# Moving the weight, token and feature buffers of a TensorE-bound layer to chosen remainders of 256 bytes

## The chip, the cores and the metric

The kernel runs on one core of a Trainium2 chip. The time is device microseconds of one execution. Three runs of the kernel before gave 2293.25, 2295.34 and 2296.85 us; the median, 2295.34 us, is the time before.

## The reference

One layer of a streaming encoder on 2048 prompt tokens and 8 x 16 sample tokens, 2176 rows of 1024 values in fp32. What matters here are its four large matrix products; between them stand two kinds of attention, norms and a gate.

```python
z = x @ w_in                                  # 1024 -> 2824
mix = concatenate([mlstm(z), window_attention(z)]) @ w_out     # 1024 -> 1024
h = layer_norm(ALPHA * x + mix)
u = h @ w_up                                  # 1024 -> 5632 (value | gate)
c = b_conv + sum(ext[:, j:j + T] * w_conv[j] for j in range(3))
y = layer_norm(ALPHA * h + (silu(gate) * value) @ w_down)      # 2816 -> 1024
```

## The kernel before

**Exactness and products.** Each fp32 operand is split into a high part that TensorE takes exactly (float32r) and the remainder, by `split` (L216 to L219): ScalarE writes the high part, VectorE the low part. A product is then three matmuls: high x high, high x low, low x high. The three largest stages (input, up and down projection) save an eighth of the blocks by a Strassen-like scheme of seven products, numbered 1 to 7, on sums and differences of quarter blocks. Where the text says "product 3", it is the `s` of the code.

**Order.** TensorE's order is written out by hand (`manual_schedule` for PE). DMAs are issued almost all on SyncE's queue. GpSimd's own queue issues 44: in the mLSTM chain a row of maxima to DRAM and back, broadcast (L1089, L1091), and 12 row blocks of the result `y` (L2133). GpSimd's transfers have a scratch in SBUF of 4096 bytes in every partition, the first thing in the memory (`dynamic_dma_scratch_size`, in `kernel`).

**Stages.**
- Input projection: four blocks of token tiles, five groups of columns. `i_product` (L701 on, matmuls at L713) streams tokens `oh`/`ol` against loaded weights `w` for groups 0 and 1 and streams weights against loaded tokens for groups 2 to 4, 256 columns each. The gate columns (264 wide) are made in `i_direct` (L739). The chains of both attentions are woven in between.
- Output projection: `group`, whose matmuls are recorded at L223 to L225 in `mm3`: the tokens are loaded, 512 columns of weights stream. One tile of 128 tokens takes eight steps of three matmuls; each two steps use one pair (high, low) of weight buffers.
- Up projection: `f_ups`, three blocks of 6, 6 and 5 token tiles. For each of 22 column tiles `j` and each product `s`, `f_product` (L1882) runs 12 matmuls: the weights `uw` are loaded, the features-to-be, tokens `hh`/`hl`, stream with 384 columns in the first two blocks and 320 in the third. The products of a round come in the order 6, 4 (of the tile before), 2, 5, 1 and 7 (of the next), 3. The PSUM banks are named `fup` and `dps` and alternate with `j`, so that products 6 | 4 | 2, 5 | 1, 7 | 3 change the name. The tokens' operands come from `f_tokens`. In the last part of the first two blocks the next block's tokens are transposed in between (L1706).
- Down projection: `f_downs` (L2090): the gated features, split into `fu` by `d_tokens`, are loaded; 512 columns of weights stream.

**Buffers.** Tiles come from pools that lie one behind the other, left to right in order of opening, and some from the right-hand end (`tsb`, later `fsb`). The slots of one tag have the size of its largest tile. The main pool `wsb` holds, after 4800 bytes of scratch and constants, four weight slots of tag `wlo`, seven raw slots of 4096 bytes and four weight slots of tag `whi`. A weight slot is 4224 bytes, because a gate tile is `[P, 2, 2, 264]` floats; all other weights fill 4096 of it. Two more slots (`wex`, 4096 bytes each) come from `wx1sb` in the output projection and from `wx2sb` in the up and down projection. In the up and down projection the ten slots are taken in turn by `f_slot`, `whi` and `wlo` alternating and the two `wex` last: an up weight's high and low half share a slot, a down weight's take two slots that follow each other.

The tokens' operands of the up projection are 6144 bytes each: `hh1`, `hl1`, `hh6`, `hl6`, `hh7`, `hl7` lie in the right-hand pool `fsb`, `hh4` and `hl4` in `f3sb`, the others in `f2sb`. `fu` uses the slots of the first six again in the down projection.

Of the kernel before, what the change touches and what calls it, by code (L numbers as in the profile page):

```python
# [8 lines left out]
F32 = mybir.dt.float32  # L9
F32R = mybir.dt.float32r  # L10
# [4 lines left out]
P = 128  # L15
# [190 lines left out]
class Prog:  # L206
# [6 lines left out]
        return self.tc.tile_pool(name=name, bufs=bufs, **kw)  # L213


    def split(self, hi, lo, src):  # L216
        nc = self.nc
        nc.scalar.copy(hi, src)  # L218
        return nc.vector.tensor_sub(lo, src, hi.bitcast(F32)).ins  # L219
# [7 lines left out]
    def run(self):  # L227
        PS = bass.MemoryType.PSUM
        nb = len(OBLOCKS)
        with ExitStack() as es:  # L230
            def enter(*a, **k):
                cm = self.pool(*a, **k)
                return cm.__enter__(), cm
            close = lambda cm: cm.__exit__(None, None, None)
            self.cp = es.enter_context(self.pool("const"))
            self.dp = es.enter_context(self.pool("dram", space=bass.MemoryType.DRAM))
            es.enter_context(self.tc.manual_schedule(engines={mybir.EngineType.PE}))
            self.setup()
            self.wp = es.enter_context(self.pool("wsb"))
            self.dps = es.enter_context(self.pool("dps", 3, PS))  # L240
            self.tp, tcm = enter("tsb", side="right")
            self.tps, tpcm = enter("tps", 5, PS)
            self.xp, xcm = enter("xsb")
            self.mp, mcm = enter("isb")
            chains = Chains(self)
            self.xs, self.gates, self.i_done = {}, {}, 0
            self.i_begin()
            self.warm_up()
            chains.weave(self.i_dense())
            close(mcm)  # L250
            wx, wxcm = enter("wx1sb")
            self.unit_more(wx)
            self.mp, mcm = enter("osb")
            self.o_setup()
            for b in range(nb - 1):
                chains.weave(self.late_done(self.o_block(b)))
            chains.until(NPT - 1)
            chains.drain()
            close(tpcm)
            close(tcm)  # L260
            self.fp, fcm = enter("fsb", side="right")
            self.fup, fpcm = enter("fup", 3, PS)
            self.f_setup()
            dense = self.o_block(nb - 1)
            first = self.f_hT(0)
            next(first)
            n = 0
            for i, _ in enumerate(dense):
                if i >= 2:
                    next(first, None)  # L270

                if i in (4, 7, 10):
                    self.f_tokens(0, *{4: (1,), 7: ("t1",), 10: ("t3", 7, "t2", 6)}[i])

                if i >= 22 and n < (2, 4, 5)[min((i - 22) // 4, 2)]:
                    self.f_next()
                    n += 1
            for _ in first:
                pass
            assert not self.norms  # L280
            close(mcm)
            close(wxcm)
            close(xcm)

            self.wx, wxcm = enter("wx2sb")
            self.f2, f2cm = enter("f2sb")
            self.f3, f3cm = enter("f3sb")
            self.f_ups(n)
            close(f3cm)
            close(f2cm)  # L290
            self.f2, f2cm = enter("d2sb")
            self.f3, f3cm = enter("d3sb")
            self.f_downs()
            for cm in (f3cm, f2cm, wxcm, fpcm, fcm):
                close(cm)
# [168 lines left out]
    def next_split(self):  # L464
        V = self.nc.vector
        if self.us >= self.ur:
            return False
        u = self.uq[self.us]
        need = 1 if u[0] == "g" else 2
        if self.halves[0] - self.halves[1] + need > self.ring:  # L470
            return False
        self.us += 1
        if u[0] == "g":
            e = self.raw_of.pop(u)
            w = self.half([P, 2, 2, 264])
            self.split(w[:, 0], w[:, 1], e[0])
            e[1] = True
            self.wu[u] = w[:, 0], w[:, 1]
            return True
        hi, lo = self.half([P, 1024]), self.half([P, 1024])  # L480
        if self.kept(u):
            for i, t in enumerate((hi, lo)):
                self.nc.sync.dma_start(t.bitcast(F32), self.zws[u[2]][SUMS.index(u[3])][i].rearrange("p a b -> p (a b)"))
        elif u[0] == "p" and u[1] == 0:
            self.split_first(u[2], u[3], hi, lo)
        else:
            e = self.raw_of.pop(u)
            self.split(hi, lo, e[0].rearrange("p a b -> p (a b)"))
            e[1] = True
        v = lambda t: t.rearrange("p (a b) -> p a b", a=2 if u[0] == "o" else 4)  # L490
        self.wu[u] = v(hi), v(lo)
        return True
# [1203 lines left out]
    def f_hT(self, b):  # L1696

        nc, fp = self.nc, self.fp
        self.hraw[b] = R = fp.tile([P, KD, 768], F32, name="hraw", tag="hraw", bufs=1)
        tiles = FBLOCKS[b]  # L1700
        hs = {}

        def transposed(ti, i, src):
            ps = self.fup.tile([P, 4, P], F32, name="fht", tag="fht", bufs=2)
            for k in range(4):
                nc.tensor.transpose(ps[:, k], src[:, k * P:(k + 1) * P], self.ident)  # L1706
            nc.scalar.copy(R[:, 4 * i:4 * i + 4, ti * P:(ti + 1) * P], ps)

        if b == 0:


            n = len(tiles) // 2
            for ts, tags in ((range(n), ("hh6", "hl6")), (range(n, 2 * n), ("hh7", "hl7"))):
                w = [fp.tile([P, 3, 512], F32, name="hst", tag=tag, bufs=1) for tag in tags]
                for c, t in enumerate(ts):
                    z = self.zh[tiles[t]].rearrange("p (i m) -> p i m", i=2)
                    at = [((2 * c + i) // 3, (2 * c + i) % 3) for i in range(2)]
                    for i, (a, k) in enumerate(at):
                        hs[t, i] = w[a][:, k]
                    if c == 1:  # L1720
                        for i, (a, k) in enumerate(at):
                            nc.scalar.dma_start(hs[t, i], z[:, i])
                    else:
                        nc.scalar.dma_start(w[at[0][0]][:, at[0][1]:at[0][1] + 2], z)
            yield
            for t, i in [(t, 0) for t in range(2 * n)] + [(t, 1) for t in (*range(n, 2 * n), *range(n))]:
                transposed(t, i, hs[t, i])
                yield
            return

        def load(ti):
            if ti < len(tiles):
                hs[ti] = fp.tile([P, D], F32, name="hst", tag="hst", bufs=2)
                nc.sync.dma_start(hs[ti], self.zh[tiles[ti]])

        for ti in range(2):
            load(ti)
        yield
        for ti in range(len(tiles)):
            for i in range(2):  # L1740
                transposed(ti, i, hs[ti][:, i * 512:(i + 1) * 512])
                if i == 1:
                    load(ti + 2)
                yield

    def f_tokens(self, b, *steps):
# [6 lines left out]
        for s in steps:  # L1753
            if s == "t1":
                V.tensor_sub(r1, r2, r1)
            elif s == "t3":
                V.tensor_sub(r2, r4, r2)
            elif s == "t2":
                V.tensor_sub(r2, r4, r1)
            elif s == "t4":  # L1760
                V.tensor_sub(r3, r3, r2)
            else:
                pool = self.fp if s in (1, 7, 6) else self.f3 if s == 4 else self.f2
                hi = pool.tile([P, 4, 384], F32R, name=f"hh{s}", tag=f"hh{s}", bufs=1)
                lo = pool.tile([P, 4, 384], F32R, name=f"hl{s}", tag=f"hl{s}", bufs=1)
                self.split(hi[:, :, :h], lo[:, :, :h], src[s])
                self.hc[b, s] = hi[:, :, :h], lo[:, :, :h]

    def f_slot(self, dt=F32R):
        self.slot = (self.slot + 1) % 10  # L1770
# [263 lines left out]
    def d_tokens(self):  # L2034
# [4 lines left out]
        b, s, u = self.dseq[self.nt]  # L2039
# [2 lines left out]
        ks = slice(DUNITS[u][0], DUNITS[u][-1] + 1)  # L2042
        n = len(DUNITS[u])
        r = {q: self.dr[b, q][:, ks, :h] for q in (1, 2, 3, 4) if (b, q) in self.dr}
        w = self.fp.tile([P, 2, 2, 384], F32R, name="fu", tag=("hh1", "hl1", "hh7", "hl7", "hh6", "hl6")[self.ring % 6], bufs=1)
        self.ring += 1
        if s == 6:
            V.tensor_sub(r[1], r[4], r[1])
# [158 lines left out]
```

## Time and profile before

| | us |
|---|---|
| median of 3 runs | 2295.34 (2293.25 to 2296.85) |
| the profiled execution | 2293.86 |
| its span, first to last instruction | 2292.1 |
| TensorE busy | 2273.5 |
| weight loads busy | 2090.7 |
| VectorE busy | 1809.8 |
| ScalarE busy | 1272.4 |
| GpSimd busy | 278.7 |

TensorE's granted clock has a mean of 0.999. HBM traffic is 274 GB/s over the span. How to read the views: PE is TensorE's matmuls, PEld its weight loads, DVE VectorE, ACT ScalarE, POOL GpSimd. In a group of instructions the names are output <- inputs, with the streamed and the loaded operand; after the count stand busy time, mean ns of one, and idle time before it. Matmuls are pipelined, so the ns of one are longer than the distance from start to start. In the chain of waits each row is a start in us, a length in us, and the work that ran then, consecutive instructions of one kind merged with their count; where TensorE is never idle the chain is TensorE's own sequence, and a row's length is how long those matmuls held it.

### The profile page before, as it was taken

How to read it: one execution, taken by the hardware profiler on the slowest of the kernel's cores; microseconds unless marked ns; L12 is line 12 of the kernel's file. 1: busy time of each engine (PE TensorE's matmuls, PEld its weight loads, DVE VectorE, ACT ScalarE, POOL GpSimd, SP SyncE). 2: the span in 40 equal slices, each digit the busy share in tenths (PEclk: the TensorE clock that was granted, in tenths of full speed). 3: DMA queues.
4: the chain of work that ended last, by engine and by line, in shares of the span. 5: the costliest groups of instructions: out<-in, count | busy, mean ns of one | idle time of the engine just before them, and what ended most of it. 6: DMA issues, size and time to landing. Idle time of an engine off the chain costs nothing.

```text
span 2292.1 us, 39775 instructions
## 1 busy us (share of the span) xinstructions
PE 2273.5 (99%) x14293; PEld 2090.7 (91%) x14293; DVE 1809.8 (79%) x3068; ACT 1272.4 (56%) x2373; POOL 278.7 (12%) x509
## 2 busy tenths in 40 slices
PE   8999999999999999999999999999999999999998
PEld 8999999999878778999999999999999988888876
DVE  8777687777788879998778777778766786895987
ACT  5453476776766656555556555555555644444442
POOL 0001001000121110211112000013111200200200
PEclk9999999999999999999999999999999999999999
DMA  8989998898998867898778999988998786757752
GB/s 283 323 305 322 316 315 276 273 313 297 333 317 263 278 219 262 314 328 299 282 269 271 302 303 306 312 265 288 324 290 264 255 292 216 254 169 224 252 157 85
DMA packets 302133, 631.30 MB, mean 275 GB/s; under 512 B 47404, under 2 KB 140656, under 8 KB 301936
## 3 DMA queue, kind: packets, MB, share of 16 engines
q1 hardware_dynamic: 297264, 615.06, 79.2%
q0 software_dynamic: 3520, 10.56, 1.5%
q10 hardware_dynamic: 1152, 3.15, 0.4%
q8 instruction: 113, 1.85, 0.3%
q14 instruction: 84, 0.69, 0.1%
HBM read 457.02 MB, written 171.64 MB: 274 GB/s over the span
## 4 chain that ended last, share of the span: by engine, by line
PE 83%; DVE 3%; issue 1%; ACT 1%; DMA 1%; POOL 0%; SPq 0%; DVEq 0%; ACTq 0%; POOLq 0%
PE dps L1882 20%; PE fup L1882 20%; PE dps L713 8%; PE fup L2090 7%; PE dps L2090 7%; PE fht L2090 6%; PE dps L223 3%; PE dps L225 2%; PE dps L224 2%; PE ppo L1359 1%; PE ppt L1353 1%; PE psc L1314 1%; PE fht L1706 1%; PE pcu L1231 1%; PE dps L739 1%
## 5 line engine op out<-in xcount | busy, mean ns | idle before, releaser
L1882 PE MATMUL fup<-hh,uw 128*128 128x384 f32 (+1 forms) x1848 | 478.2, 328 | 0.0
L1882 PE MATMUL dps<-hh,uw 128*128 128x384 f32 (+1 forms) x1848 | 478.0, 328 | 0.0
L1882 PEld LDWEIGHTS fup<-hh,uw 128*128 128x128 f32 x1848 | 330.2, 188 | 0.0
L1882 PEld LDWEIGHTS dps<-hh,uw 128*128 128x128 f32 x1848 | 330.1, 188 | 0.0
L1882 PE MATMUL fup<-hl,uw 128*128 128x384 f32 (+1 forms) x924 | 302.9, 328 | 1.0 <-DVE hl L219 1.0
L1882 PE MATMUL dps<-hl,uw 128*128 128x384 f32 (+1 forms) x924 | 302.7, 328 | 0.0
L1940 DVE SCALAR_TENSOR_TENSOR cc<-u,cw,cc 128x768 f32<-128x768 f32 (+1 forms) x264 | 258.0, 978 | 39.3 <-ACT cc L1938 30.8
L713 PE MATMUL dps<-w,oh 128*128 128x256 f32 x1344 | 254.8, 285 | 0.1
L218 ACT CAST uw<-wraw 128x1024 fp32r<-128x1024 f32 x126 | 123.3, 978 | 228.2 <-PE dps L2090 122.2
L219 DVE TENSOR_TENSOR w<-wraw,w 128x1024 fp32r<-128x1024 f32 (+2 forms) x163 | 186.0, 1149 | 61.6 <-ACT w L218 58.6
L218 ACT CAST w<-wraw 128x1024 fp32r<-128x1024 f32 (+2 forms) x163 | 160.2, 992 | 113.8 <-PE dps L713 53.7
L713 PEld LDWEIGHTS dps<-w,oh 128*128 128x128 f32 x1344 | 210.9, 188 | 11.2 <-issue 8.1
L219 DVE TENSOR_TENSOR uw<-wraw,uw 128x1024 fp32r<-128x1024 f32 x126 | 142.2, 1129 | 61.2 <-ACT uw L218 61.2
L713 PE MATMUL dps<-w,ol 128*128 128x256 f32 x672 | 188.2, 280 | 0.0
L1882 PEld LDWEIGHTS fup<-hl,uw 128*128 128x128 f32 x924 | 173.7, 188 | 1.7 <-DVE hl L219 1.6
L1882 PEld LDWEIGHTS dps<-hl,uw 128*128 128x128 f32 x924 | 173.7, 188 | 0.0
L2090 PE MATMUL fup<-uw,fu 128*128 128x512 f32 x726 | 173.6, 396 | 0.0
L713 PE MATMUL dps<-oh,w 128*128 128x256 f32 x896 | 168.0, 283 | 3.9 <-DVE w L219 2.2
L2090 PEld LDWEIGHTS fup<-uw,fu 128*128 128x128 f32 x726 | 136.5, 188 | 32.7
L2090 PE MATMUL dps<-uw,fu 128*128 128x512 f32 x660 | 164.8, 396 | 0.0
L2090 PEld LDWEIGHTS dps<-uw,fu 128*128 128x128 f32 x660 | 124.1, 188 | 29.8
L713 PEld LDWEIGHTS dps<-oh,w 128*128 128x128 f32 x896 | 140.0, 188 | 10.1 <-issue 4.1
(320 smaller groups left out, 4567.6 us busy)
## 6 DMA issues: line engine op xcount, KB each, us to landing
uw<-zw SPq DMA_DIRECT2D x176, 512.0 KB, 5.0
zw<-uw SPq DMA_DIRECT2D x88, 512.0 KB, 3.3
w<-zws SPq DMA_DIRECT2D x72, 512.0 KB, 6.0
wv<-wup SPq DMA_DIRECT2D x66, 512.0 KB, 5.2
wraw<-wi SPq DMA_DIRECT2D x65, 512.0 KB, 5.2
wraw<-zt SPq DMA_DIRECT2D x60, 512.0 KB, 4.3
wraw<-wdn SPq DMA_DIRECT2D x45, 512.0 KB, 4.9
wraw<-wo SPq DMA_DIRECT2D x40, 512.0 KB, 5.1
```

The lines of the kernel that those rows point to most:

```text
L218: nc.scalar.copy(hi, src)
L219: return nc.vector.tensor_sub(lo, src, hi.bitcast(F32)).ins
L223: mm(out, ah, bh, start=start, stop=False)
L224: mm(out, ah, bl, start=False, stop=False)
L225: mm(out, al, bh, start=False, stop=stop)
L713: mm(o, l, r, start=s in (1, 7) and c == k == i == 0, stop=k == 3 and i == 2, skip_group_check=True)
L739: mm(o, x, w, start=k == i == 0, stop=k == KD - 1 and i == 2, skip_group_check=True)
L1231: nc.tensor.matmul(ps[:, i], kw[:, h], v1[:, h], start=True, stop=True)
L1314: nc.tensor.matmul(ps[kvh][:, j, :nk], q[rs, j0 + j], k[rs, sel], start=i == 0, stop=i == 2)
L1882: mm(ps, l[:, k], r[:, k], start=s in (1, 7) and k == 0 and i == 0, stop=k == 3 and i == 2, skip_group_check=True)
L1940: V.scalar_tensor_tensor(c[:, v], u[:, i:i + n], w[i], c[:, v], op0=ALU.mult, op1=ALU.add)
L2090: mm(ps, l[:, k, c], r[:, k], start=s in (1, 4, 7) and u == 0 and k == 0 and i == 0, stop=u == nu - 1 and k == n - 1 and i == 2, skip_grou ...
```

## The change

No instruction is added or taken away on any engine; buffers move.

- The scratch of GpSimd's transfers is 1024 instead of 4096 bytes in each partition; all left-hand pools move down by that.
- The gate tile is allocated with 272 columns, of which 264 are used: a weight slot is 4352 bytes, 17 x 256. Scratch and constants now end at 1728 = 6 x 256 + 192.
- An unused tile of 192 bytes (`pad`) opens `wx1sb` and `wx2sb`, one of 64 opens `f2sb`, one of 192 opens `f3sb`, and one of 224 is added to `fsb`.
- `f_buf` allocates the operands of the up projection, and the token rows that share their slots, as flat tiles. In `fsb` such a tile has 256 bytes to spare, and `fu` begins 56 floats (224 bytes) into it.

```diff
+    def pad(self, pool, n):
+        pool.tile([P, n // 4], F32, name="pad", tag="pad", bufs=1)
...
             wx, wxcm = enter("wx1sb")
+            self.pad(wx, 192)
...
             self.wx, wxcm = enter("wx2sb")
+            self.pad(self.wx, 192)
             self.f2, f2cm = enter("f2sb")
+            self.pad(self.f2, 64)
             self.f3, f3cm = enter("f3sb")
+            self.pad(self.f3, 192)
+            self.pad(self.fp, 224)
             self.f_ups(n)
...
-            w = self.half([P, 2, 2, 264])
+            w = self.half([P, 2, 2, 272])[:, :, :, :264]
...
-                w = [fp.tile([P, 3, 512], F32, name="hst", tag=tag, bufs=1) for tag in tags]
+                w = [self.f_buf(fp, F32, "hst", tag, [3, 512]) for tag in tags]
...
-                hi = pool.tile([P, 4, 384], F32R, name=f"hh{s}", tag=f"hh{s}", bufs=1)
-                lo = pool.tile([P, 4, 384], F32R, name=f"hl{s}", tag=f"hl{s}", bufs=1)
+                hi, lo = [self.f_buf(pool, F32R, f"{n}{s}", f"{n}{s}", [4, 384]) for n in ("hh", "hl")]
...
+    def f_buf(self, pool, dt, name, tag, shape, at=0):
+
+        t = pool.tile([P, 1536 + (64 if pool is self.fp else 0)], dt, name=name, tag=tag, bufs=1)[:, at:at + 1536]
+        d = dict(zip("abc", shape[:-1]))
+        return t.rearrange(f"p ({' '.join(d)} m) -> p {' '.join(d)} m", **d)
...
-        w = self.fp.tile([P, 2, 2, 384], F32R, name="fu", tag=("hh1", "hl1", "hh7", "hl7", "hh6", "hl6")[self.ring % 6], bufs=1)
+        w = self.f_buf(self.fp, F32R, "fu", ("hh1", "hl1", "hh7", "hl7", "hh6", "hl6")[self.ring % 6], [2, 2, 384], 56)
...
-    nc = bacc.Bacc("TRN2", target_bir_lowering=False, num_devices=1, dynamic_dma_scratch_size=4096)
+    nc = bacc.Bacc("TRN2", target_bir_lowering=False, num_devices=1, dynamic_dma_scratch_size=1024)
```

## The prediction

> **What bounds the kernel now.** I read the page's busy times first, then TensorE's waits, then the stages, then the chain of waits product by product.
>
> ```profile
> span 2292.1 us, 39775 instructions
> PE 2273.5 (99%) x14293; PEld 2090.7 (91%) x14293; DVE 1809.8 (79%) x3068; ACT 1272.4 (56%) x2373; POOL 278.7 (12%) x509
> ...
> L1882 PE MATMUL fup<-hh,uw 128*128 128x384 f32 (+1 forms) x1848 | 478.2, 328 | 0.0
> ...
> L2090 PE MATMUL fup<-uw,fu 128*128 128x512 f32 x726 | 173.6, 396 | 0.0
> ```
> ```profile
> PE dps L713 <- DVE w L219: 2.2, 2, 1.4
> PE dps L328 <- DVE zero L323: 2.0, 1, 2.0
> PE ppt L1526 <- POOL v L1104: 1.4, 1, 1.4
> ```
>
> TensorE is busy for 99% of the span, and its three longest kinds of wait come to 5.6 us. So only its own pace, the time from one matmul's start to the next, can move the end by much: a matmul is recorded with 328 or 396 ns, but they overlap, and the pace is less. The stages show it (TensorE's busy time, then its matmuls in brackets; then weight loads, VectorE, ScalarE, GpSimd):
>
> ```profile
> 20.10:615.40 595.30, 589.33 (x5044) 560.09 (x5044) 443.50 (x1006) 362.01 (x793) 44.82 (x70) 1.00 0.90 304
> 616.00:892.70 276.70, 276.52 (x1530) 217.18 (x1529) 238.33 (x555) 173.44 (x418) 45.70 (x49) 1.00 0.81 272
> 893.00:1222.10 329.10, 328.70 (x1900) 327.89 (x1898) 284.61 (x406) 194.61 (x325) 54.46 (x90) 1.00 0.80 293
> 1222.10:1545.60 323.50, 322.94 (x1865) 322.30 (x1865) 240.66 (x284) 173.01 (x271) 36.92 (x88) 1.00 0.89 295
> 1549.20:1820.90 271.70, 271.70 (x1851) 271.70 (x1850) 198.98 (x286) 148.89 (x279) 60.00 (x178) 1.00 0.88 286
> 1821.30:2283.50 462.20, 462.02 (x1981) 371.75 (x1980) 380.30 (x487) 203.47 (x260) 31.86 (x29) 1.00 0.63 209
> ```
>
> These are: the input projection, the output projection, the up projection's three blocks, the down projection. The granted clock is full (1.00) in all. In the up blocks TensorE has no gap (328.70 of 329.10), and VectorE has 44 us of 329 free in the first, 83 of 323 in the second. So a shorter matmul there ends the block earlier by as much.
>
> **Does the pace depend on addresses?** The change moves buffers and nothing else, so this is the question. Where an operand begins is worked out by laying the pools out in the order in which the code allocates them. Before, with 4096 bytes of scratch, the eight weight slots of the main pool are 4224 bytes apart from 4800 on (7 x 4096 of raw slots between): remainders of 256 are 192, 64, 192, 64 in both tags. The extra pair (`wex`, 67584 and 71680) has remainder 0. The up projection's token operands have 224 (`hh1`, `hh6`, `hh7`), 64 (`hh4`) and 0 (`hh2`, `hh3`, `hh5`). A weight takes the next of ten slots, seven are taken per round, so every product meets each kind of slot over ten rounds. In the chain of waits of the second block the products stand one by one (start, length, bank, 12 matmuls; two products that follow each other on one bank are one row of 24):
>
> ```profile
> 1252.39 2.10 PE dps L1882 x12
> 1254.49 2.12 PE fup L1882 x12
> 1256.61 2.11 PE dps L1882 x12
> 1258.72 4.17 PE fup L1882 x24
> ...
> 1267.06 2.11 PE fup L1882 x12
> ...
> 1281.75 2.08 PE dps L1882 x12
> ...
> 1285.93 2.08 PE dps L1882 x12
> ...
> 1296.38 2.08 PE fup L1882 x12
> ...
> 1300.56 2.11 PE fup L1882 x12
> ...
> 1315.20 2.08 PE dps L1882 x12
> ...
> 1327.80 2.09 PE dps L1882 x12
> ...
> 1342.45 2.12 PE fup L1882 x12
> ...
> 1344.57 2.12 PE dps L1882 x12
> ...
> 1384.40 2.08 PE fup L1882 x12
> ```
>
> Call the offset the start of the streamed operand less that of the loaded one, mod 256; here tokens stream and weights are loaded. Product 3 (1267.06, 1281.75, 1296.38, 1384.40) has tokens at 0: on weights at 0 it lasts 2.11 us, on weights at 192, offset 64, it lasts 2.08 each of three times. Product 6 has tokens at 224: on weights at 192, offset 32, 2.12 (1254.49, 1342.45); on weights at 0, offset 224, 2.09 (1327.80). Product 4 has tokens at 64: on weights at 192, offset 128, 2.11 and 2.12 (1300.56, 1344.57); on weights at 0, which is offset 64 again, 2.08 (1285.93); at offset 0 it lasts 2.11 in one row (1256.61) and 2.08 in another (1315.20). So the pace goes largely by the offset: 64 is the quick one, 32 and 128 are slow, 0 is mixed. The two of 1258.72, products 2 and 5 on weights at 192, take 2.085 each. From 1252.39 to 1384.40, nine whole rounds, 63 products take 132.01 us: 2.0954 each.
>
> In the third block, with 320 columns, nothing of this is seen:
>
> ```profile
> 1562.35 1.76 PE fup L1882 x12
> ...
> 1574.68 1.77 PE dps L1882 x12
> ```
>
> **The change part by part.** Laid out anew: scratch 1024 puts the first weight slot at 1728, remainder 192; gate tiles of 272 columns make the slot 4352 bytes, a multiple of 256, so all eight keep 192; the pads of 192 bring both `wex` pools there too. The pads of 64, 192 and 224 with the 6400-byte slots of the right-hand pool put every `hh` and `hl` at 0; `fu` at 56 floats past them is at 224.
>
> *Up projection, 384 columns.* All 308 products (2 x 22 x 7) of the first two blocks get tokens at 0 and weights at 192, the quick pairing. The rows of it average (3 x 2.08 + 4.17) / 5 = 2.082; 2.0954 − 2.082 = 0.0134 us, times 308 is −4.1 us. Ends: 2.075 and 2.0875, as rounded rows allow, give −6.3 and −2.4.
>
> *Up projection, 320 columns.* 1.76 in all pairings: 0.
>
> *Down projection.* Here the weights stream and the tokens (`fu`) are loaded. `fu` stays at 224; weights go from 64 (four tenths), 192 (four) and 0 (two) to 192.
>
> ```profile
> 1903.36 2.80 PE fht L2090 x12
> ...
> 1907.56 2.79 PE fht L2090 x12
> ...
> 1936.91 2.81 PE fht L2090 x12
> ```
>
> Every product mixes a high and a low half in different slots, or has both in the extra pair, so no row here has what comes. By offset the up rows stand 64 (2.08), 224 (2.09), 32 (2.12). Two tenths of the 1980 matmuls go from 32 to 224: 0.03 / 12 = 2.5 ns each, 396 times, −1.0 us. Four tenths go from 96 to 224; 96 isn't among the rows, its neighbours 64 and 128 (2.08, 2.115) allow nothing to 2.5 ns, half of it is −1.0 us. Four tenths stay. I take −2.0. Ends: the quickest 12 matmuls of 512 columns anywhere are the 2.77 below, 230.8 ns each against 462.2 / 1980 = 233.4, which gives −5.1; the slowest row above, 2.81, is 234.2 ns, +1.6.
>
> *Output projection.* The weights stream, tokens at 0 are loaded; this is not made to fit by the change. By start of every third matmul:
>
> ```profile
> 801.75 0.39 PE L223 MATMUL dps<-w,oh 128*128 128x512 f32 x1
> ...
> 804.52 0.40 PE L223 MATMUL dps<-w,oh 128*128 128x512 f32 x1
> ...
> 807.34 0.40 PE L223 MATMUL dps<-w,oh 128*128 128x512 f32 x1
> ...
> 808.74 0.39 PE L223 MATMUL dps<-w,oh 128*128 128x512 f32 x1
> ```
>
> Four threes on a pair at 64 and 192 take 804.52 − 801.75 = 2.77, 0.6925 each; two threes on a pair both at 192 take 1.40, 0.700 each. One pair in five is of the second kind now, all 272 threes (17 tiles, 2 halves, 8 steps) will be: 0.0075 x 272 x 4/5 = +1.6 us. Ends: 0 and double.
>
> *Input projection.* Two of five groups load the weights, three stream them, so 192 against 0 stands there in both orders; no row resolves a class. I take 0, within 1.5 us each way (0.45 ns on each of 3360 matmuls). The gate weights' rows, now 1088 bytes apart, are 408 matmuls in it.
>
> *Splits, evictions, loads.* ScalarE and VectorE write the same elements to other starts, and the transfers land at other remainders. I take nothing for it: what covers it is the free 44 to 83 us of VectorE in the blocks, and without that cover each us of it would be a us of the end.
>
> *GpSimd's scratch.* Its own queue has few transfers, close together only in pairs:
>
> ```profile
> 1971.32 0.61 POOL L2133 DMA_DIRECT2D y<-yacc  x1 [4.15 <-DVE yacc L2132]
> 1972.13 0.55 POOL L2133 DMA_DIRECT2D y<-yacc  x1 [0.20 <-issue]
> 1977.31 3.47 POOL L1567 TENSOR_TENSOR lsc<-lsc,mhalf 128x1 f32<-128x1 f32 x1 [4.63 <-DVE lsc L1566]
> ```
> ```profile
> y<-yacc POOLq DMA_DIRECT2D x12, 512.0 KB, 4.4
> ```
>
> If a quarter of the scratch held one transfer only, the second of a pair would wait until the first lands, 4.4 us after 1971.32; the next thing on GpSimd starts at 1977.31. So 0. The Trainium skill's page DMA: Bandwidth & Descriptors (SWDGE vs HWDGE vs iDMA, and Terms) puts 16-byte descriptors into rings in this carveout; 1024 bytes would by an estimate from that hold 64 a ring, and no row shows a ring's fill.
>
> Sum: −4.1 − 2.0 + 1.6 + 0 = −4.5 us, on an execution of 2293.86 us; the median of the runs is 1.5 us above it, and the sum is laid on the median: 2295.34 − 4.5 = 2290.8 us (−0.20%).
>
> **The rivals.**
>
> *A: the start doesn't matter.* The lengths would belong to where in the round a product stands, and the time stays 2295.3. Against it: product 3 alone, on one place, has 2.08 and 2.11. The Trainium skill (TensorE: Matmul & The Clock Gate, Part 2, Step-by-step) says that TensorE has two independent read ports, so that loading the next weights doesn't take read bandwidth from the running matmul; by that rule the sum is 0. The rows of product 3 disagree with it, by 0.03 us in 2.1.
>
> *B: the down projection finds its quick pairing.* It gets the pace of the 2.77 row: −4.1 − 5.1 + 1.6 = −7.6, 2287.7; with the input projection's 1.5, 2286.2. For it: 1980 matmuls of one fixed offset, 224, quick in product 6 (2.09). Against: no 512-column row has it.
>
> *C: weights at 192 are slow wherever the tokens now aren't at 0.* Then 2.12 belongs to the products 6, 1, 7 and 4 and to the slot, not to the offset. These four (176 products) go from 2.10 to 2.115, +2.6; products 2, 3, 5 (132) gain 0.01 each, −1.3; the output projection's +1.6 stays; the down projection takes the slow rows' excess, 462 x (2.12 / 2.0954 − 1) = +5.4. Sum +8.3: 2303.6. It decides once product 6 with tokens at 0 still shows 2.12. Product 4's 2.08 with weights at 0 against 2.12 at 192 can be read this way too; product 3's 2.08 at 192 can't.
>
> **How the numbers follow.** A measurement of this kernel tells about 0.2% from no change, 4.6 us. My forecast 0.50, its own range 2287 to 2294; 0.32 of it lies beyond 4.6 us, more than half, since the down projection's ends reach further that way (−5.1 against +1.6). B 0.22; A, or gains that the output and input projections eat, 0.17; C 0.11. Faster: 0.32 + 0.22 = 0.54; same: 0.18 + 0.17 = 0.35; slower 0.11. The range reaches from B with the up projection's far end (2286.2 − 2.2 = 2284) to past A and the spread of the runs: 2284 to 2297.
>
> **What the profile after would show.** Right: rows of 12 all at 2.08 in the first two up blocks, also for products 6 and 4, the nine rounds in about 131.2 us; 1.76 in the third; the down projection's window at about 460 us; output projection 1 to 2 us longer; no new wait of TensorE, none on GpSimd's transfers. Wrong: any row of 2.11 or 2.12 left, a down row of 2.82, or a wait behind VectorE in the first block, where it has least to spare.

## The result and the profile after

The changed kernel takes 2289.95 us (median of 18 runs, 2287.65 to 2293.38) against 2294.02 us (18 runs, 2292.70 to 2296.85): 4.1 us less, a ratio of 0.998 with a 95% interval of 0.9974 to 0.9987.

The page of the kernel after; its lines are up to 13 further down; L1895 is the up projection, L2103 the down projection:

```profile
span 2289.5 us, 39775 instructions
PE 2269.4 (99%) x14293; PEld 2083.6 (91%) x14293; DVE 1808.9 (79%) x3068; ACT 1272.9 (56%) x2373; POOL 275.5 (12%) x509
...
L1895 PE MATMUL fup<-hh,uw 128*128 128x384 f32 (+1 forms) x1848 | 476.9, 327 | 0.2 <-ACT ub L1924 0.2
...
L2103 PE MATMUL fup<-uw,fu 128*128 128x512 f32 x726 | 173.8, 396 | 0.0
```

The counts are the same and VectorE and ScalarE are as busy as before (1808.9 against 1809.8, 1272.9 against 1272.4). TensorE's waits, longest first, are the same three as before:

```profile
PE dps L721 <- DVE w L222: 2.2, 2, 1.3
PE dps L336 <- DVE zero L331: 2.0, 1, 2.0
PE ppt L1534 <- POOL v L1112: 1.4, 1, 1.4
```

The stages of before and after, cut at the first matmul of each (input, output, the three up blocks, down to its last matmul); the number after the bounds is the length. Before:

```profile
20.15:615.98 595.83, 589.86 (x5047) 560.04 (x5045) 443.73 (x1007) 362.54 (x793) 44.82 (x70) 1.00 0.90 304
615.98:893.07 277.09, 276.91 (x1531) 217.49 (x1530) 238.70 (x556) 173.46 (x418) 45.70 (x49) 1.00 0.81 272
893.07:1222.10 329.03, 328.63 (x1899) 327.86 (x1897) 284.54 (x406) 194.61 (x325) 54.46 (x90) 1.00 0.80 293
1222.10:1549.20 327.10, 326.54 (x1890) 325.90 (x1889) 244.26 (x287) 176.46 (x275) 40.22 (x89) 1.00 0.89 294
1549.20:1821.36 272.16, 272.16 (x1853) 272.07 (x1851) 199.44 (x287) 149.35 (x280) 60.46 (x179) 1.00 0.88 286
1821.36:2283.32 461.96, 461.78 (x1981) 371.74 (x1979) 380.24 (x487) 203.41 (x260) 31.80 (x28) 1.00 0.63 209
```

After:

```profile
20.55:614.97 594.42, 588.33 (x5046) 558.49 (x5044) 443.89 (x1007) 362.35 (x793) 43.96 (x70) 1.00 0.91 305
614.97:894.24 279.27, 278.38 (x1531) 217.14 (x1530) 238.67 (x556) 174.15 (x418) 44.93 (x49) 1.00 0.81 270
894.24:1220.63 326.39, 326.11 (x1899) 325.33 (x1898) 283.54 (x406) 194.65 (x325) 53.31 (x90) 1.00 0.81 295
1220.63:1545.68 325.05, 324.35 (x1890) 323.70 (x1889) 244.30 (x287) 176.24 (x275) 40.40 (x89) 1.00 0.90 296
1545.68:1818.27 272.59, 272.40 (x1853) 272.05 (x1851) 199.44 (x287) 149.33 (x280) 61.91 (x179) 1.00 0.89 285
1818.27:2280.71 462.44, 462.27 (x1981) 371.38 (x1979) 379.97 (x487) 203.51 (x260) 29.79 (x29) 1.00 0.63 209
```

So the input projection is 1.4 us shorter, the output projection 2.2 longer, the up blocks 2.6 and 2.1 shorter and 0.4 longer, the down projection 0.5 longer: −3.0 us together. The spans differ by 2.6 us (2292.1 and 2289.5). The medians differ by 4.1; what lies between is of the size of the input stage's spread: it took 592.8 to 594.4 us in this execution and the six below that share its offsets there. (The profiled execution itself took 2291.27 us, that of before 2293.86.)

The nine rounds that the prediction read, and three single products (3, 6 and 4 in turn) of the kernel after, as stretches:

```profile
1250.72:1381.76 131.04, 131.04 (x757) 131.04 (x757) 97.25 (x117) 68.69 (x108) 12.04 (x36) 1.00 0.92 308
1250.72:1252.80 2.08, 2.08 (x13) 2.08 (x13) 2.04 (x3) 0.62 (x1) 0.00 (x0) 1.00 0.59 208
1252.80:1254.88 2.08, 2.08 (x13) 2.08 (x13) 0.96 (x2) 1.88 (x3) 0.19 (x1) 1.00 1.04 356
1254.88:1256.96 2.08, 2.08 (x13) 2.08 (x13) 1.90 (x2) 0.53 (x2) 0.00 (x0) 1.00 0.99 376
```

131.04 / 63 = 2.080 us each, and product 6, which stood at 2.12 or 2.09, and product 4, at 2.11 or 2.08, take 2.08 like product 3. (A stretch counts 13 matmuls, since one from before its start is still running.) The down projection stands where it did:

```profile
1904.53 2.80 PE fht L2103 x12
...
1910.83 2.79 PE fht L2103 x12
...
1915.02 2.80 PE fht L2103 x12
```

### The profile page after: what moved, and what is told of

Its sections match the earlier page's. It is cut to its first block, busy times and chain, and to the rows that moved or that the text cites. A ratio compares the mean times of both kernels' runs of the same rounds, so it can differ in the third digit from the quotient of the medians.

```text
span 2289.5 us, 39775 instructions
## 1 busy us (share of the span) xinstructions
PE 2269.4 (99%) x14293; PEld 2083.6 (91%) x14293; DVE 1808.9 (79%) x3068; ACT 1272.9 (56%) x2373; POOL 275.5 (12%) x509
## 5 line engine op out<-in xcount | busy, mean ns | idle before, releaser
L1895 PE MATMUL fup<-hh,uw 128*128 128x384 f32 (+1 forms) x1848 | 476.9, 327 | 0.2 <-ACT ub L1924 0.2
L1895 PE MATMUL dps<-hh,uw 128*128 128x384 f32 (+1 forms) x1848 | 476.7, 327 | 0.0
L1895 PEld LDWEIGHTS fup<-hh,uw 128*128 128x128 f32 x1848 | 329.1, 188 | 0.5 <-ACT ub L1924 0.4
L1895 PEld LDWEIGHTS dps<-hh,uw 128*128 128x128 f32 x1848 | 329.1, 188 | 0.0
L1895 PE MATMUL fup<-hl,uw 128*128 128x384 f32 (+1 forms) x924 | 301.9, 327 | 1.0 <-DVE hl L222 1.0
L1895 PE MATMUL dps<-hl,uw 128*128 128x384 f32 (+1 forms) x924 | 301.6, 326 | 0.0
L1895 PEld LDWEIGHTS fup<-hl,uw 128*128 128x128 f32 x924 | 173.6, 188 | 1.7 <-DVE hl L222 1.6
L2103 PE MATMUL fup<-uw,fu 128*128 128x512 f32 x726 | 173.8, 396 | 0.0
L1895 PEld LDWEIGHTS dps<-hl,uw 128*128 128x128 f32 x924 | 173.6, 188 | 0.0
L2103 PEld LDWEIGHTS fup<-uw,fu 128*128 128x128 f32 x726 | 136.4, 188 | 33.0
L2103 PE MATMUL dps<-uw,fu 128*128 128x512 f32 x660 | 165.0, 396 | 0.0
L2103 PEld LDWEIGHTS dps<-uw,fu 128*128 128x128 f32 x660 | 124.0, 188 | 30.0
```

The lines of the kernel that those rows point to most:

```text
L1895: mm(ps, l[:, k], r[:, k], start=s in (1, 7) and k == 0 and i == 0, stop=k == 3 and i == 2, skip_group_check=True)
L2103: mm(ps, l[:, k, c], r[:, k], start=s in (1, 4, 7) and u == 0 and k == 0 and i == 0, stop=u == nu - 1 and k == n - 1 and i == 2, skip_grou ...
```

## The experiments

The theory: a matmul's pace follows the offset, the start of the streamed operand less that of the loaded one, mod 256. The rivals: place and product set it (A), the weights' own remainder sets it (C), or the smaller scratch and the plain move do.

**The scratch alone**, on the kernel before:

```diff
-dynamic_dma_scratch_size=4096
+dynamic_dma_scratch_size=1024
```

> The kernel before with GpSimd's scratch of 1024 bytes alone: every left-hand pool moves down by 3072 bytes, 12 x 256, so all remainders of 256 stay as they were. Offset theory (pace follows streamed start less loaded start, mod 256): every stage as before within 0.3 us, up blocks 329.0 and 327.1 us, time within 0.1% of the kernel before. If the scratch or the plain address counts: the up blocks go part of the way to 326.4 and 325.1 us, or GpSimd's transfers show a wait.

2294.64 us beside 2294.16 us for the kernel before. Both up blocks and the down projection:

```profile
892.48:1221.49 329.01, 328.62 (x1899) 327.84 (x1897) 284.65 (x406) 194.69 (x325) 53.22 (x90) 1.00 0.80 293
1221.49:1548.60 327.11, 326.56 (x1890) 325.91 (x1890) 244.27 (x287) 176.23 (x275) 40.34 (x89) 1.00 0.89 294
1822.12:2284.11 461.99, 461.81 (x1980) 371.35 (x1979) 380.23 (x487) 203.38 (x260) 25.80 (x29) 1.00 0.63 209
```

They are within 0.03 us of before (329.03, 327.10, 461.96). The left-hand pools have moved by 12 x 256 bytes and the right-hand one has not, so plain addresses and distances differ from before and the remainders do not. Neither that shift nor the smaller scratch does anything to these stages. (The input projection, 594.98, and the third up block, 273.53, miss the 0.3 us that were expected, by 0.6 and 1.1; in the third block TensorE waited once for ScalarE, 1.1 us.)

**Everything by 64**, on the changed kernel: weights at 0, tokens at 64, features at 32.

```diff
             self.wp = es.enter_context(self.pool("wsb"))
+            self.pad(self.wp, 64)
...
-    def f_buf(self, pool, dt, name, tag, shape, at=0):
-
+    def f_buf(self, pool, dt, name, tag, shape, at=None):
+        at = at if at is not None else 16 if pool is self.fp else 0
...
-        w = self.f_buf(self.fp, F32R, "fu", ..., [2, 2, 384], 56)
+        w = self.f_buf(self.fp, F32R, "fu", ..., [2, 2, 384], 8)
```

> The changed kernel with weights, tokens and features all 64 bytes further: weights at 0, tokens at 64, features at 32; each offset stays as in the changed kernel. Offset theory: the stages of the changed kernel again (input 594.4, output 279.3, up 326.4 and 325.1, down 462.4 us, each within 0.4 us). Rival that the remainders themselves count (192 for weights or 0 for tokens): the up products leave 2.080 us, by 5 ns or more, and the up blocks lengthen by 1 us or more.

```profile
890.72:1217.10 326.38, 326.10 (x1899) 325.30 (x1898) 283.63 (x406) 194.61 (x325) 53.16 (x90) 1.00 0.80 295
1217.10:1542.15 325.05, 324.35 (x1889) 323.70 (x1889) 244.32 (x287) 176.25 (x275) 40.39 (x89) 1.00 0.90 296
1814.74:2277.20 462.46, 462.29 (x1981) 371.36 (x1979) 380.27 (x487) 203.26 (x260) 25.80 (x29) 1.00 0.63 209
```

The changed kernel's 326.39, 325.05 and 462.44 again, with no start at its old remainder. The time, 2287.72 us, lies within the spread of the changed kernel's runs. (Input, 592.78, and output, 278.10, are 1.6 and 1.2 us below the figures expected, more than the 0.4 allowed; the runs below that keep the changed kernel's offsets there take 593.5 to 594.4 and 278.1 to 279.2, so 0.4 was too narrow for these two stages.) In the up and down projection it is the offset and not the remainders; C, where the weights' slot would decide, falls with this and with product 6 at 2.08 above. That 256 is the right divisor, and not 512, shows in the changed kernel itself: its weight slots are 17 x 256 bytes apart, so that the offset mod 512 is 64 on one slot and 320 on the next, and the products take 2.080 us on both.

**Products 1, 6 and 7 back to tokens at 224**, on the changed kernel, so that their offset is 32:

```diff
-    def f_buf(self, pool, dt, name, tag, shape, at=0):
-
+    def f_buf(self, pool, dt, name, tag, shape, at=None):
+        at = at if at is not None else 56 if pool is self.fp else 0
```

> The changed kernel with the operands of products 1, 6 and 7 at 224 and all else as it is: offset 32 for these three, 64 for the other four. Offset theory: products 1, 6, 7 last 2.115 us in the first two blocks (as in the rows of before with that offset) and 2, 3, 4, 5 stay at 2.080; 132 x 0.035 us = 4.6 us longer up blocks. Rival that starts don't matter but product and place do: all rows stay at 2.08, up blocks 326.4 and 325.1 us.

2293.82 us. One round in the chain of waits (3 | 6 | 4 | 2, 5 | 1, 7):

```profile
1252.19 2.08 PE dps L1896 x12
1254.27 2.12 PE fup L1896 x12
1256.39 2.08 PE dps L1896 x12
1258.47 4.16 PE fup L1896 x24
1262.63 4.24 PE dps L1896 x24
```

The three that were moved take 2.12 each, the others stay. The two blocks take 328.52 and 327.02 us, 4.1 us more than in the changed kernel; 4.6 were expected. The products' places are the same in both kernels, so A falls.

One exception tells more. In 11 of the 44 rounds the transposes of the next block's tokens stand just before products 1 and 7, and there these two take the quick 4.16 us, though their offset is still 32 (a round without transposes, then one with):

```profile
1066.21 4.24 PE fup L1896 x24
...
1080.90 0.44 PE fht L1714 x4
1081.33 4.16 PE dps L1896 x24
```

So at offset 32 there are two paces, and a break in the sequence can bring the other one. By the starts in the trace, 110 of the 132 moved products are slow; at 0.04 us each that is 4.4 us, close to the 4.1 measured. At offset 64 there is one pace: of the changed kernel's 282 products with another straight behind them, 258 last 2.080 us, and 22 of the other 24 stand just behind the transposes.

**The features at 192**, on the changed kernel, offset 0 in the down projection:

```diff
-        w = self.f_buf(self.fp, F32R, "fu", ..., [2, 2, 384], 56)
+        w = self.f_buf(self.fp, F32R, "fu", ..., [2, 2, 384], 48)
```

> The changed kernel with the features 192 past, as the weights: offset 0 in the down projection instead of 224. Before, the output projection's threes at offset 0 took 690 ns against 699 at 192, 230 ns a matmul. Offset theory: the down projection's 1980 matmuls go from 233.4 to about 230 ns, 6 us shorter (456 us), the rest unchanged. Rival that 512 columns don't care and 233.4 is the floor in this stage: 462 us.

2276.53 us beside 2294.16. The down projection, and rows of its chain of waits:

```profile
1816.24:2265.99 449.75, 449.54 (x1981) 370.96 (x1979) 378.34 (x487) 204.17 (x260) 31.82 (x29) 1.00 0.65 215
```
```profile
1895.99 2.72 PE fht L2103 x12
1898.71 1.36 PE dps L2103 x6
1900.08 2.72 PE fht L2103 x12
```

Twelve matmuls take 2.72 us instead of 2.80 and the stage is 12.7 us shorter, twice what was expected. TensorE was the bound there too, and 32 bytes decide over 2.7% of the stage.

**Two more offsets in the down projection**: features at 0 (`at` 0, offset 192) and at 128 (`at` 32, offset 64), the same line of the code.

> The changed kernel with the features at 0: offset 192 in the down projection. The output projection runs at offset 192 with the same 512 columns and takes 700 ns for three. Offset theory: 233.3 ns a matmul here too, the down projection 462 us. If only equal starts (offset 0, 226.8 ns) or the remainder of the features counts: another figure, up to 6 ns away from the output projection's.

> The changed kernel with the features at 128: offset 64 in the down projection. The up projection is quickest at 64 (2.080 us for 12 matmuls of 384 columns, 173.3 ns or 13.3 more than 384 / 2.4), the output projection's threes at 64 took 694 ns before. If the quick offset is the same for every width: 226.8 ns (13.5 over 512 / 2.4) and 450 us. If it depends on the width: about 231 ns as in the output projection, 458 us.

Features at 0, then features at 128:

```profile
1817.40:2279.84 462.44, 462.27 (x1981) 371.26 (x1979) 380.08 (x487) 203.48 (x260) 29.82 (x29) 1.00 0.63 209
```
```profile
1818.33:2272.21 453.88, 453.68 (x1981) 371.21 (x1979) 379.37 (x487) 203.81 (x260) 29.81 (x29) 1.00 0.64 213
```

At offset 192 the 1980 matmuls take 462.44 us, 233.6 ns each, as at 224; the output projection's 233.3 is met. At 64 they take 453.88, 229.2 ns, between the two answers expected (226.8 and 231). So the quick offset isn't one for all widths: 64 is best of those seen for 384 columns, 0 for 512. (In uniform sequences 384 columns were seen at 64 and 32 only. That with 512 columns the offset counts and not the remainders was tested at 224 alone, by the shift of everything by 64.)

**Token operands of input and output projection at 192 too**, with the features at 192: offset 0 there.

```diff
             self.xp, xcm = enter("xsb")
+            self.pad(self.xp, 192)
...
             wx, wxcm = enter("wx1sb")
-            self.pad(wx, 192)
```

> The changed kernel with the features at 192 and the token operands of input and output projection at 192 as well: offset 0 in input, output and down projection, 64 in the up projection. Offset theory: the output projection's threes go from 700 to 690 ns or, as the down projection did, to 680: 3 to 5 us shorter than 279; the down projection stays at 449.8 us; the input projection is the open one, offset 0 was never seen there with 256 columns: between all groups at the quick 680 ns per six (about 5 us shorter) and all at 707 (4 us longer). Rival that the output projection is held by the chains woven into it: 279 us stays.

2287.15 us. Input and output projection:

```profile
21.31:625.05 603.74, 598.99 (x5047) 569.55 (x5045) 444.32 (x1007) 363.05 (x794) 44.64 (x70) 1.00 0.89 300
625.05:901.70 276.65, 275.66 (x1531) 217.37 (x1530) 238.09 (x556) 173.52 (x417) 45.09 (x49) 1.00 0.81 272
```

The output projection, 512 columns, gains 2.6 us on the changed kernel (expected 3 to 5). The input projection, 256 columns, loses 9.3, more than the worst expected: by the starts in the trace its sixes (six matmuls in a row) come to a median of 720 ns whichever operand streams. What is best for one width is bad for another.

**The kernel of the features at 192, timed:**

> The kernel of e4 again (features at 192), timed against the kernel before in rounds. Offset theory: e4's down projection is 12.7 us shorter than the changed kernel's (449.75 against 462.44 us) and the changed kernel is 4.1 us faster than before, so 2294.0 - 4.1 - 12.7 = 2277 us, ratio 0.9927. Rival that the one time of e4 was luck: 2284 us or more.

2277.67 us (5 runs, 2276.55 to 2278.37) against 2293.97 us (9 runs): ratio 0.993, interval 0.9916 to 0.9943. It beats both kernels, the changed one by 12.3 us of medians.

**Token operands at 32 and at 64**, features at 192 (`pad(self.xp, 32)` with `pad(wx, 160)`, and 64 with 128):

> As e4, with the token operands of input and output projection at 32: offset 160 where weights stream (input groups 2 to 4, output), 96 where tokens stream (input groups 0 and 1). With 256 columns, sixes took 689 ns at offset 192, 705 at 64, 720 at 0. Offset theory: each figure moves with the offset and is the same for all of its kind; which way isn't known, 680 is the quickest seen. The output projection leaves its 700 ns for three. Rival: these stages don't follow the offset, and only equal starts hurt: 689, 705 and 700 stay.

> As e4, with the token operands of input and output projection at 64: offset 128 whichever operand streams. Offset theory: both kinds of the input projection's sixes come to one figure, as they did at offset 0 (720 and 719 ns), wherever it lies. Rival that it matters which operand is the weights and not the offset: the two kinds differ by 10 ns or more, as they do at 192 and 64.

2284.57 and 2284.47 us. Tokens at 32, then at 64, input projection:

```profile
20.21:621.51 601.30, 596.59 (x5046) 566.93 (x5044) 443.99 (x1007) 362.92 (x794) 44.66 (x70) 1.00 0.89 301
```
```profile
20.14:621.88 601.74, 596.73 (x5046) 567.00 (x5044) 444.03 (x1007) 363.86 (x794) 44.63 (x70) 1.00 0.88 301
```

Both are 7 to 9 us longer than the 592.8 to 594.4 us with tokens at 0. By the starts in the trace, the sixes at 64, where the offset is 128 in either order, have a median of 713 ns with weights streamed and 714 with tokens streamed; at 32, where the offsets are 160 and 96, it is 709 and 720. So in the input projection too the offset counts, and not which operand is the weights. The output projection was expected to leave its 700 ns for three and hardly does: the median is 703 in both, and the stage takes 278.6 us with tokens at 32 and 278.7 at 64, within the 278.1 to 279.3 that it has with tokens at 0.

With 256 columns, though, one offset can have two paces, as 32 has with 384. In the changed kernel all sixes with the weights streamed are at offset 192; of the 219 undisturbed ones (another six straight behind) 146 take 680 ns and 69 take 707. Here are ten sixes of each kind:

```profile
107.01:113.81 6.80, 6.80 (x62) 6.80 (x61) 6.80 (x10) 3.46 (x5) 0.00 (x0) 1.00 0.89 284
225.63:232.70 7.07, 7.07 (x63) 7.07 (x61) 2.65 (x4) 3.02 (x7) 0.59 (x1) 1.00 1.01 313
```

With the tokens streamed, at offset 64, the same two lengths occur, 707 in 137 of 143. Taking both orders, the length stayed the same from one six to the next in all 272 cases without a break, and changed over 15 of 70 breaks. So the offset goes with which lengths occur and how often; what picks one after a break, no run here shows.

## Why the prediction was right, and where it was wrong

2290.8 us was forecast and 2289.95 measured; −4.5 us against −4.1. (The forecast was laid on a median of three runs, 2295.34 us; that of 18 is 2294.02.) The mechanism in the up projection was the one argued, but the sum came so close by luck: terms that were off partly cancel. The terms measured are differences of the two profiled executions, −3.0 us in all:

- *Up projection, 384 columns: −4.1 forecast, −4.7 measured* (2.64 + 2.05). The reading by offset was right: every product at 2.080, nine rounds in 131.04 us against 131.2. It is the main cause of the gain: putting three products back lengthened the two blocks by 4.1 us again.
- *Up projection, 320 columns: 0 forecast, +0.4.* Within what the stage varies by (271.9 to 274.3 in the runs).
- *Down projection: −2.0 forecast, +0.5 measured.* This step failed, though inside its ends. It took the order of the offsets from 384 columns (224 at 2.09 better than 32 at 2.12) over to 512, where 224 is no quick offset: it takes the same 233.6 ns as 192. (32 and 96, which the matmuls left, were not run alone with 512 columns.) It also took the weights' slots as if each matmul had its own price. Before, by the starts in the trace, a matmul with weights at 192 held TensorE for 232.1 ns, one at 64 for 234.0, one at 0 for 233.4; with all at 192 the same offset takes 233.4. So a matmul's length in a mixed sequence depends on its neighbours too, and the price of a uniform sequence can't be read from the members of a mixed one. The up projection had uniform products, twelve matmuls on one offset, and there the reading held for the quick offset.
- *Output projection: +1.6 forecast, +2.2 measured*, for the reason given, offset 192 throughout; at offset 0 it is 2.6 us shorter.
- *Input projection: 0 within 1.5 forecast, −1.4 measured.* By the starts in the trace, sixes with the weights streamed fell from 704 to 689 ns (mean of the undisturbed) and sixes with the tokens streamed rose from 690 to 706. Both orders moved, against each other, as the text had left open; these means are mostly shares of 680 and 707.
- *Scratch, splits, evictions, loads: 0 forecast.* For the scratch the run with it alone shows it. For the rest, VectorE's and ScalarE's busy times are as before, and TensorE's three longest waits are the same.

Rival B had the right idea and the wrong offset: the down projection has a quick pairing, 227.1 ns (449.75 / 1980), quicker than the 230.8 that B took from the output projection, but it is offset 0 and not 224. Rival A would have left every stage as it was; here the same dozen matmuls takes 2.08 or 2.12 us with 384 columns and 2.72 or 2.80 with 512, after nothing but starts were moved. The rule beside it, that loading the next weights takes no read bandwidth from the running matmul (the Trainium skill, TensorE: Matmul & The Clock Gate, Part 2, Step-by-step), gives no such difference. Why the starts count, no run here shows.

## What to carry to other kernels

Where TensorE never waits, look at the length of a dozen equal matmuls in the chain of waits: if it steps between a few values, compare the starts of streamed and loaded operand mod 256, and try the offsets of each stage apart, because the best one of those seen depends on the number of columns (64 for 384, 0 for 512, 192 for 256). Read such a price only from sequences that are uniform in the offset, and from many of them, since one offset can have two paces. A sweep of the offset in one stage is one constant in the code and is worth more than a choice by argument: here 32 bytes were worth three times the whole change.

## What was not expected of the hardware

- The offset moves the pace by 2 to 3%: with 384 columns 2.080 us (offset 64) to 2.120 (32) for twelve matmuls; with 512 columns, the stage divided by its matmuls, 227.1 ns (0), 229.2 (64), 233.6 (192 and 224) for one; with 256 columns the input projection takes 593 to 594 us (192 and 64), 601 (160 and 96), 602 (128) or 604 (0). With 320 columns next to nothing was seen (1.75 to 1.77 us for twelve at all offsets of before).
- One offset can have two paces (2.08 or 2.12 us for twelve of 384 columns at 32; 680 or 707 ns for six of 256 columns at 192 and 64), and in the input projection a sequence kept the one that it had until a break.
- Equal starts are the quickest seen with 512 columns, and with 256 columns they give the longest stage seen.
- At a uniform good offset the products lose their scatter: in the nine rounds they last 2.080 us, where before they lay between 2.08 and 2.12.
